# One group per expert for transposes, way back, scatter and gather; 4-KB pieces for gate and up rows

## The chip, the cores and the metric

The kernel runs on 1 core of one Trainium2 chip. The metric is device time in microseconds (us) of one execution; a kernel's time is the median over its runs. Engines are named as the profile names them: PE (TensorE matmul), PEld (TensorE weight load), DVE (VectorE), ACT (ScalarE), POOL (GpSimd), SP (SyncE, which issues nearly all DMAs).

## What is computed

256 positions of width 1024 pass through two blocks of two layers each. The first block and the attention parts of the second are untouched; the change lies in the mixture of experts that ends each layer of the second block:

```python
def grouped_moe(x, w_router, b_router, w_gate, w_up, w_down):
    scores = softmax(x @ w_router + b_router)
    ...  # group of 4 experts with the largest top-2 sum, then top 2 experts in it, renormalised -> gate (256, 16)
    y = zeros_like(x)
    for e in range(16):
        h = silu(x @ w_gate[e]) * (x @ w_up[e])      # 1024 -> 512
        y = y + gate[:, e:e+1] * (h @ w_down[e])     # 512 -> 1024
    return y
```

followed by `x = layer_norm(sqrt(2) * x + y)`. All weights are float32; one expert has 6.3 MB of them.

## The kernel before

**Weights.** All weights of the kernel come as one list of units of 512 KB in the order of their use. `load_ahead` (L262) issues the load of the next unit on SP as soon as a room (a 512-KB buffer in SBUF) is free in program order; `close` gives rooms back after the matmuls that read them. `hold(n)` keeps the next n rooms that come free away from the loads, and `take` hands them out for other tiles. An expert has 12 units: 4 pairs of gate and up (two blocks k of 128 rows by 512 columns each, so 2 KB in one piece) and 4 of down (128 rows by 1024 columns, 4 KB in one piece). The expert weights are used as they land, without the split into two parts that the other weights get.

**Router and gather.** `router` computes gates and, for each expert, a place among at most 64 (`CAP`) for each of its positions. `greater` and `lesser` split x into two parts `xn` for exact gathering. `gather(q)` makes `xgs[q]`, the transposed inputs of the four experts of group q: `select(q)` builds the one-hot `pick` on DVE, then four pieces of 8 matmuls each (L1845) go into a bank and are copied out by ACT or DVE in turn. Gather 0 runs ahead of the experts, gathers 1 to 3 are generators that `tick` moves on between units of the experts' matmuls.

**Experts.** `into(e)` multiplies the 64 gathered rows by gate and up: 4 steps u of two k each; gate goes to rows 0 to 63 of a bank and up to rows 64 to 127, so that the two matmuls use the two column halves of the array (64 columns each, L1936). `turn(e)` transposes the result (4 transposes, L1950), ACT applies silu (L1952), DVE multiplies (L1953). `down(e)` multiplies by the down weights (L1961), and ACT and DVE evict the result in two parts (L1967, L1968). `way_back(e)` makes the matrix that scatters back: POOL `pk` (L1862), 2 transposes (L1867), two DVE operations (L1870, L1871). `scatter(e)` adds the result to the four accumulators with 8 matmuls (L1977).

**Order.** The engines run in program order, written out by hand. The loop takes into(e+1) and then down(e). `turn(e)` is hooked behind step u = 0 of into(e+1), `scatter(e-1)` behind u = 2, `way_back(e+1)` comes by ticks behind u = 3, and pieces of a gather lie between steps. In experts 1, 4 and 8 a gather is started, and all its four pieces fall into into(e+1).

**Banks.** PSUM has 8 banks: 4 accumulators, and here 3 of kind `mm` (into, down) and 1 of kind `tp` (turn, way_back, gather). All tp users thus share one bank, each waiting until the one before has been read out. In layer 0, `memory` also uses tp late in the loop: from e = 12 it loads `stage` from ACT's queue and transposes it for the next layer.

Of the kernel before, what the change touches and what calls it, by code (L numbers as in the profile page):

```python
# [69 lines left out]
def the_kernel(  # L70
# [194 lines left out]
    def load_ahead(upto=None):  # L265
        units, loads, spare = now["units"], now["loads"], now["spare"]
        while spare and len(spare) > wanted_spare():
            give([spare.pop()])
        while len(loads) < min(len(units), upto or len(units)) and free:
            at = free.pop(0)  # L270
            w, c0, n, k0, m, _, _ = units[len(loads)]
            r = block(at, [UNIT], name="raw")[:, :m * n].rearrange("p (k n) -> p k n", n=n)
            nc.sync.dma_start(r, w[k0 * P:(k0 + m) * P, c0:c0 + n].rearrange("(k p) n -> p k n", p=P))
            loads.append((r, at))
            now["busy"].append(at)
# [1375 lines left out]
    def memory_attention(l, cs, xt, ready, memT, KT):  # L1651
        (memT, mem_rooms), (KT, KT_rooms) = memT, KT
        nxt, renew = start_norm(l, 1, split=False)
        with tc.tile_pool(name=f"xa{l}", bufs=1, reuse_waits="tile") as mp:
# [52 lines left out]
            gs = out_product(ot, renew, *([[gs[j, h]] for h in range(NH)] for j in range(2)), hurry=True)  # L1707
            hold(4)
            give(V_rooms + qT_rooms + KT_rooms + o_rooms)
            return nxt, gs  # L1710

    def moe(l, cs, xt, ready, turns, less_room):
        xg_rooms, xn_rooms = [], take(4, 4)
        xT = lambda h, k: xt[k // 4][:, k % 4, h * P:(h + 1) * P]
        later, whole, before, ones, numbers, order, earlier, alpha, wr, tr, sp = cs
        with tc.tile_pool(name=f"moe{l}", bufs=1, reuse_waits="tile") as mp:
# [6 lines left out]

            xn = [[block(r, [D], FR, "xn") for r in xn_rooms[i::2]] for i in range(2)]

            def greater(h):

                for j in range(2):
                    nc.scalar.activation(xn[0][h][:, j * 512:(j + 1) * 512], x[h][j], AF.Copy)

            def lesser(h, j):
                hi, lo = (t[h][:, j * 512:(j + 1) * 512] for t in xn)
                nc.vector.tensor_sub(lo, x[h][j], hi.bitcast(FT))

# [96 lines left out]
            def gather(q):  # L1831
# [3 lines left out]
                pick = picks[q]  # L1835
                if q % 2:
                    xg_rooms.extend(take(2, 2))
                xgs[q] = [block(r, [4, 4, CAP], name="xg") for r in (xg_rooms if q % 2 else pair_rooms[:2])]
                yield from wait(GW[0] if q else 0)
                for i in range(4):  # L1840
                    p = bank("tp" if q else "mm").rearrange("p (k e s) -> p k e s", k=2, s=CAP)
                    for k in range(2):
                        for h in range(NH):
                            for part in range(2):
                                nc.tensor.matmul(p[:, k].rearrange("p e s -> p (e s)"),  # L1845
                                                 xn[part][h][:, (2 * i + k) * P:(2 * i + k + 1) * P],
                                                 pick[:, h].rearrange("p e s -> p (e s)"), start=h == part == 0,
                                                 stop=h == part == 1)
                    o = xgs[q][i // 2][:, i % 2 * 2:i % 2 * 2 + 2]
                    if i % 2:  # L1850
                        nc.vector.tensor_copy(o, p)
                    else:
                        nc.scalar.activation(o, p, AF.Copy)  # L1853
                    yield from wait(2 if q else 0)
                if q == 3:
                    give(xn_rooms)

            def way_back(e):
# [5 lines left out]
                yield from wait(WB)  # L1864
# [3 lines left out]
                bk = mp.tile([P, NH, P], FR, name="back", bufs=2)  # L1868
                gw = mp.tile([P, 1], FT, name="gw", bufs=2)
# [3 lines left out]
                yield  # L1873

# [110 lines left out]
            turns.close()  # L1985
            turns.enter_context(banks(mm=3, tp=1))
            nc.scalar.activation(t2()[:, :1], gates[:, 0, 0:1], AF.Silu)
# [9 lines left out]

            spawn(way_back(0))
            into(0)
            for e in range(16):  # L2000
                if e in (0, 6):
                    hold(2)
                if e in (7, 15):
                    give(xg_rooms)
                    xg_rooms.clear()
                if e in (1, 4, 8):
                    gs.append(spawn(gather(len(gs))))
                if e == ME[0] and l == 0:
# [10 lines left out]
                if e == 15:  # L2019
# [4 lines left out]
                    break  # L2024
                if e % 4 == 3:
                    finish(gs[-1])
                wt = spawn(way_back(e + 1))
                into(e + 1, {0: lambda: turn(e), 2: lambda: e and scatter(e - 1)})
                finish(wt)
                down(e, (lambda: turn(15)) if e == 14 else None)  # L2030
# [91 lines left out]
```

## Time and profile before

| | |
|---|---|
| median of 3 runs | 2220.94 us (2216.73 to 2223.05) |
| profiled execution | 2218.42 us, its span 2216.7 us |
| PE busy, share of the span | 2132.8 us, 96% |
| DVE, ACT, POOL busy | 1139.0, 910.7, 177.0 us |
| HBM read | 487.34 MB |
| the largest PE groups of the experts | L1936 242.7 us (x1024), L1961 119.3 us (x512) |

Where rows show a time line, the columns are start, duration (from the first start to the last end of a merged group), engine, line, operation, out<-in, partitions*columns of the weights, the operand's shape, count and, in brackets, idle time of the engine before it and what ended it. A float32 matmul of the experts is recorded as two, so that a step u has 8 records of L1936 and down has 16 of L1961. Matmul ends are modelled; starts are the safer number. Rows of windows give the busy time of each engine, the granted clock, the DMA share and GB/s.

### The profile page before, as it was taken

Reading aid. Unit: us, or ns where it says so; the run is one execution under the profiler, and the core shown is the slowest. Engines: PE = TensorE matmul, PEld = TensorE weight load, DVE = VectorE, ACT = ScalarE, POOL = GpSimd, SP = SyncE. Lnnn points to the kernel's source line nnn. Section 1 sums busy time; section 2 is a strip of 40 time slices with the busy share of each in tenths; the row PEclk is TensorE's granted clock in tenths of the full one; section 3 lists DMA queues with packets and bytes.
Section 4 is the critical chain, followed back from the end, with each engine's and each line's share of the span. In section 5 each row is a group of like instructions: output and inputs, shape, how many; then the busy total and the mean of one; then the engine's idle time right before and its main releaser. Section 6 shows DMA issues by size and latency. Waiting matters only on the chain. (4 is left out here: it accounts for less than half of the span.)

```text
span 2216.7 us, 29473 instructions
## 1 busy us (share of the span) xinstructions
PE 2132.8 (96%) x11117; PEld 1569.8 (71%) x11117; DVE 1139.0 (51%) x2022; ACT 910.7 (41%) x1448; POOL 177.0 (8%) x230
## 2 busy tenths in 40 slices
PE   8999989999999999899999999998999999989997
PEld 7778878788888888788788887873333687953332
DVE  6545786654554547875554457651111558441112
ACT  5435655454454447564544454531111454421111
POOL 1000200200000002101100001101000102010000
PEclk9999999999999999999999999999999999999999
DMA  7655553555546555535666464778998946589996
GB/s 249 195 177 153 163 153 110 175 183 186 181 156 210 188 172 154 162 105 158 224 205 194 153 186 159 249 251 307 393 394 300 353 126 219 185 308 381 395 393 246
DMA packets 240076, 490.49 MB, mean 221 GB/s; under 512 B 17538, under 2 KB 44850, under 8 KB 239922
## 3 DMA queue, kind: packets, MB, share of 16 engines
q1 hardware_dynamic: 239634, 487.42, 65.1%
q8 instruction: 92, 1.51, 0.3%
q10 hardware_dynamic: 288, 1.05, 0.1%
q14 instruction: 62, 0.51, 0.1%
HBM read 487.34 MB, written 1.07 MB: 220 GB/s over the span
## 5 line engine op out<-in xcount | busy, mean ns | idle before, releaser
L285 DVE TENSOR_TENSOR wlo<-raw,whi 128x1024 fp32r<-128x1024 f32 x524 | 633.8, 1227 | 300.7 <-ACT whi L311 297.9
L311 ACT ACTIVATE whi<-raw 128x1024 fp32r<-128x1024 f32 x524 | 540.7, 1051 | 299.8 <-PE tp L360 117.5
L1936 PE MATMUL mm<-raw,xg 128*64 128x512 f32 x1024 | 242.7, 602 | 7.9 <-PEq L1992 7.2
L358 PE MATMUL accB<-whi,xt 128*128 128x512 f32 (+3 forms) x448 | 176.2, 393 | 0.0
L360 PE MATMUL accB<-whi,xt 128*128 128x512 f32 (+3 forms) x448 | 166.0, 370 | 0.0
L359 PE MATMUL accB<-wlo,xt 128*128 128x512 f32 (+3 forms) x448 | 165.8, 370 | 0.0
L1936 PEld LDWEIGHTS mm<-raw,xg 128*64 128x64 f32 x1024 | 69.6, 137 | 132.8 <-issue 121.5
L358 PE MATMUL tp<-whi,xt 128*128 128x512 f32 (+1 forms) x384 | 143.4, 373 | 0.0
L360 PE MATMUL tp<-whi,xt 128*128 128x512 f32 (+1 forms) x384 | 143.4, 373 | 0.0
L359 PE MATMUL tp<-wlo,xt 128*128 128x512 f32 (+1 forms) x384 | 142.7, 372 | 0.0
L358 PE MATMUL mm<-whi,xt 128*128 128x512 f32 (+1 forms) x320 | 121.0, 378 | 1.4 <-DVE nbias L720 0.7
L1961 PE MATMUL mm<-raw,t 128*64 128x512 f32 x512 | 119.3, 607 | 0.5 <-DMA raw<-in_w_down_dram 0.5
L360 PE MATMUL mm<-whi,xt 128*128 128x512 f32 (+1 forms) x320 | 118.3, 370 | 0.0
L359 PE MATMUL mm<-wlo,xt 128*128 128x512 f32 (+1 forms) x320 | 117.7, 368 | 0.0
L1941 ACT ACTIVATE t<-mm 128x512 f32<-128x512 f32 x32 | 19.1, 597 | 187.5 <-PE mm L1936 187.5
L360 PEld LDWEIGHTS accB<-whi,xt 128*128 128x128 f32 x448 | 84.5, 189 | 15.1
L358 PEld LDWEIGHTS accB<-whi,xt 128*128 128x128 f32 x448 | 84.6, 189 | 13.6 <-issue 1.0
L359 PEld LDWEIGHTS accB<-wlo,xt 128*128 128x128 f32 x448 | 84.8, 189 | 11.8
L1870 DVE TENSOR_SCALAR back<-tp 128x256 fp32r<-128x256 f32 x32 | 13.6, 424 | 149.2 <-PE tp L1867 149.2
L610 DVE SCALAR_TENSOR_TENSOR t<-tp,ss,t 128x512 f32<-128x512 f32 (+1 forms) x48 | 33.8, 704 | 104.2 <-PE tp L360 104.2
L359 PEld LDWEIGHTS tp<-wlo,xt 128*128 128x128 f32 x384 | 72.1, 188 | 13.5
L360 PEld LDWEIGHTS tp<-whi,xt 128*128 128x128 f32 x384 | 72.1, 188 | 13.2
(520 smaller groups left out, 4007.7 us busy)
## 6 DMA issues: line engine op xcount, KB each, us to landing
raw<-in_w_gate_dram SPq DMA_DIRECT2D x128, 512.0 KB
raw<-in_w_up_dram SPq DMA_DIRECT2D x128, 512.0 KB
raw<-in_w_down_dram SPq DMA_DIRECT2D x128, 512.0 KB
raw<-in_w_in_dram SPq DMA_DIRECT2D x120, 512.0 KB
raw<-in_ffn_w_gate_dram SPq DMA_DIRECT2D x88, 512.0 KB
raw<-in_ffn_w_up_dram SPq DMA_DIRECT2D x88, 512.0 KB
raw<-in_ffn_w_down_dram SPq DMA_DIRECT2D x88, 512.0 KB
raw<-in_w_out_dram SPq DMA_DIRECT2D x32, 512.0 KB
```

The source lines that it names most:

```text
L285: eng.tensor_sub(lo, r, hi.bitcast(FT))
L311: nc.scalar.activation(hi, r, AF.Copy)
L358: nc.tensor.matmul(o, xh, wh, start=first, stop=False)
L359: nc.tensor.matmul(o, xh, wl, start=False, stop=False)
L360: nc.tensor.matmul(o, xl, wh, start=False, stop=last)
L610: nc.vector.scalar_tensor_tensor(ss[h], o, factor(h), ss[h], op0=OP.mult, op1=OP.mult)
L1870: nc.vector.tensor_scalar(bk, tp, 0.0, None, op0=OP.is_gt)
L1936: nc.tensor.matmul(p[half(i)], xgs[e // 4][k // 4][:, k % 4, e % 4], W.whole(k, i), start=k == 0, stop=k == KD - 1)
L1941: nc.scalar.activation(c[e], p, AF.Copy)
L1961: nc.tensor.matmul(p[half(j)], uu[e][:, f], W.whole(f)[:, j * 512:(j + 1) * 512], start=f == 0, stop=f == 3)
```

## The change

- `between` is hooked behind u = 1 of into(e+1) and holds, in this order: turn(e), way_back(e+1), scatter(e-1), and one piece of a gather. The POOL part of way_back is now `gated_places`, issued ahead of into. Nothing is hooked behind u = 0, 2 and 3 any more.
- Gather 1 starts ahead of into(0), gathers 2 and 3 at e = 3 and 7; each puts one piece into each of four groups.
- Banks: 2 of mm and 2 of tp (3 and 1 before). `back` and `gw` have 3 buffers (2 before).
- The two rooms for odd gathers are taken once at the start of `moe` (`hold(6)` in place of `hold(4)`) and kept to e = 15; before, they were held at e = 0 and 6 and given back at e = 7 and 15.
- Gate and up units: partition p now gets rows 8p + k, so that its two rows k, k + 1 are neighbours in HBM: one piece of 4 KB where there were two of 2 KB, 16 KB from one partition's piece to the next. To match, `xn` holds the columns of x in the order k, m (from 8m + k), so that `greater` and `lesser` read x with a step of 8 elements.

```diff
-            w, c0, n, k0, m, _, _ = units[len(loads)]
+            w, c0, n, k0, m, _, whole = units[len(loads)]
             r = block(at, [UNIT], name="raw")[:, :m * n].rearrange("p (k n) -> p k n", n=n)
-            nc.sync.dma_start(r, w[k0 * P:(k0 + m) * P, c0:c0 + n].rearrange("(k p) n -> p k n", p=P))
+            if whole and m > 1:
+                nc.sync.dma_start(r, w[:, c0:c0 + n].rearrange("(p k) n -> p k n", p=P)[:, k0:k0 + m])
+            else:
+                nc.sync.dma_start(r, w[k0 * P:(k0 + m) * P, c0:c0 + n].rearrange("(k p) n -> p k n", p=P))
...
-            hold(4)
+            hold(6)
...
-        xg_rooms, xn_rooms = [], take(4, 4)
+        xg_rooms, xn_rooms = take(2, 2), take(4, 4)
...
+            eighths = lambda t, j: t.rearrange("p (k m) -> p k m", k=KD)[:, :, j * 64:j * 64 + 64]
...
-                    nc.scalar.activation(xn[0][h][:, j * 512:(j + 1) * 512], x[h][j], AF.Copy)
+                    nc.scalar.activation(eighths(xn[0][h], j), x[h][j].rearrange("p (m k) -> p k m", k=KD), AF.Copy)
...
-                yield from wait(GW[0] if q else 0)
                 for i in range(4):
+                    if i or q:
+                        yield
...
-                    yield from wait(2 if q else 0)
...
-            turns.enter_context(banks(mm=3, tp=1))
+            turns.enter_context(banks(mm=2, tp=2))
...
-            spawn(way_back(0))
-            into(0)
+            pk = gated_places(0)
+            rest_of = gather(1)
+            next(rest_of)
+            into(0, {1: lambda: (way_back(0, pk), next(rest_of))})
             for e in range(16):
...
-                if e in (1, 4, 8):
-                    gs.append(spawn(gather(len(gs))))
+                if e in (3, 7):
+                    rest_of = gather(e // 4 + 2)
+                    next(rest_of)
...
-                wt = spawn(way_back(e + 1))
-                into(e + 1, {0: lambda: turn(e), 2: lambda: e and scatter(e - 1)})
-                finish(wt)
+                pk = gated_places(e + 1)
+                def between():
+                    turn(e)
+                    way_back(e + 1, pk)
+                    if e:
+                        scatter(e - 1)
+                    next(rest_of, None)
+                into(e + 1, {1: between})
                 down(e, (lambda: turn(15)) if e == 14 else None)
```

## Rows read from the trace of the kernel before

**Rows 1.** Part 2 of the page: GB/s in 40 slices of 55.4 us

```profile
GB/s 249 195 177 153 163 153 110 175 183 186 181 156 210 188 172 154 162 105 158 224 205 194 153 186 159 249 251 307 393 394 300 353 126 219 185 308 381 395 393 246
```

**Rows 2.** Time line of PE, one expert of layer 1 without a gather

```profile
2017.03 1.89 PE L1936 MATMUL mm<-raw,xg 128*64 128x512 f32 x8
2018.85 0.66 PE L1950 MATMUL tp<-ident,t 128*128 128x128 f32 x4
2019.44 3.65 PE L1936 MATMUL mm<-raw,xg 128*64 128x512 f32 x16
2023.02 0.73 PE L1977 MATMUL accA<-t,back 64*128 64x512 f32 x4
...
2024.15 1.94 PE L1936 MATMUL mm<-raw,xg 128*64 128x512 f32 x8
2026.02 0.44 PE L1867 MATMUL tp<-ident,pk 128*128 128x128 f32 x2
2026.38 3.65 PE L1961 MATMUL mm<-raw,t 128*64 128x512 f32 x16
2029.87 1.89 PE L1936 MATMUL mm<-raw,xg 128*64 128x512 f32 x8
```

**Rows 3.** Time line of PE, the gather ahead of layer 1's experts and expert 1's

```profile
1970.99 4.05 PE L1845 MATMUL mm<-pick,xn 128*128 128x256 f32 x32
...
1997.60 1.89 PE L1936 MATMUL mm<-raw,xg 128*64 128x512 f32 x8
...
2001.13 1.21 PE L1845 MATMUL tp<-pick,xn 128*128 128x256 f32 x8 [1.06 <-DVE t L1953]
...
2008.28 1.21 PE L1845 MATMUL tp<-pick,xn 128*128 128x256 f32 x8
2010.17 1.21 PE L1845 MATMUL tp<-pick,xn 128*128 128x256 f32 x8 [0.69 <-ACT xg L1853]
```

**Rows 4.** Time line of PE, first group and end of layer 1's experts

```profile
1988.11 0.41 PE L1867 MATMUL tp<-ident,pk 128*128 128x128 f32 x2 [1.07 <-DVE t L1953]
...
2196.70 4.71 PE L1961 MATMUL mm<-raw,t 128*64 128x512 f32 x20
...
2203.03 0.49 PE L1977 MATMUL accA<-t,back 64*128 64x512 f32 x2 [0.26 <-DVE t L1968]
```

**Rows 5.** L273 on SP, 1979.5 to 2185: count, ns min/median/max, first and last start

```profile
L273 SPq DMA_DIRECT2D raw<-in_w_down_dram x56: 327/334/716, 1981.8 to 2181.6; - x56
L273 SPq DMA_DIRECT2D raw<-in_w_up_dram x50: 367/378/741, 1979.6 to 2170.8; - x50
L273 SPq DMA_DIRECT2D raw<-in_w_gate_dram x49: 367/383/1456, 1980.1 to 2169.5; - x49
```

**Rows 6.** Windows: start:end, length, PE, PEld, DVE, ACT, POOL, clock, DMA, GB/s

```profile
2134.50:2135.00 0.50, 0.50 (x6) 0.41 (x4) 0.00 (x0) 0.00 (x0) 0.00 (x0) 1.00 1.03 410
...
2158.50:2159.00 0.50, 0.50 (x6) 0.14 (x2) 0.00 (x0) 0.39 (x1) 0.00 (x0) 1.00 1.05 389
...
2190.00:2194.00 4.00, 4.00 (x24) 1.70 (x24) 0.51 (x2) 0.60 (x1) 0.00 (x0) 1.00 0.67 267
1742.00:1748.00 6.00, 5.06 (x38) 4.54 (x38) 5.86 (x13) 1.93 (x3) 1.60 (x1) 1.00 1.08 381
```

**Rows 7.** Time lines of SP, ACT and PE, end of layer 0's experts

```profile
1669.10 21.62 SPq L273 DMA_DIRECT2D raw<-in_w_down_dram  x4
...
1684.45 1.89 PE L1936 MATMUL mm<-raw,xg 128*64 128x512 f32 x8
...
1684.82 1.11 ACTq L1358 DMA_DIRECT2D stage<-in_mem_dram  x2
...
1697.09 1.08 PE L1961 MATMUL mm<-raw,t 128*64 128x512 f32 x4 [0.47 <-DMA raw<-in_w_down_dram]
...
1734.64 4.72 PE L1961 MATMUL mm<-raw,t 128*64 128x512 f32 x20
```

**Rows 8.** Groups by line, DVE in 1480 to 1500 us

```profile
L1733 DVE TENSOR_TENSOR xn<-x,xn 128x512 fp32r<-128x512 f32 x4 | 2.6, 677 | 0.0
```

More of the change, by code (lines that the diff above doesn't have):

```diff
@@ L1724, in moe @@
             xn = [[block(r, [D], FR, "xn") for r in xn_rooms[i::2]] for i in range(2)]
+            eighths = lambda t, j: t.rearrange("p (k m) -> p k m", k=KD)[:, :, j * 64:j * 64 + 64]
             def greater(h):
                 for j in range(2):
-                    nc.scalar.activation(xn[0][h][:, j * 512:(j + 1) * 512], x[h][j], AF.Copy)
+                    nc.scalar.activation(eighths(xn[0][h], j), x[h][j].rearrange("p (m k) -> p k m", k=KD), AF.Copy)
             def lesser(h, j):
-                hi, lo = (t[h][:, j * 512:(j + 1) * 512] for t in xn)
-                nc.vector.tensor_sub(lo, x[h][j], hi.bitcast(FT))
+                hi, lo = (eighths(t[h], j) for t in xn)
+                nc.vector.tensor_sub(lo, x[h][j].rearrange("p (m k) -> p k m", k=KD), hi.bitcast(FT))
             def router():
@@ L1835, in gather @@
                 pick = picks[q]
-                if q % 2:
-                    xg_rooms.extend(take(2, 2))
                 xgs[q] = [block(r, [4, 4, CAP], name="xg") for r in (xg_rooms if q % 2 else pair_rooms[:2])]
-                yield from wait(GW[0] if q else 0)
                 for i in range(4):
+                    if i or q:
+                        yield
                     p = bank("tp" if q else "mm").rearrange("p (k e s) -> p k e s", k=2, s=CAP)
@@ L1853, in gather, with gated_places @@
                         nc.scalar.activation(o, p, AF.Copy)
-                    yield from wait(2 if q else 0)
                 if q == 3:
                     give(xn_rooms)
-            def way_back(e):
+                yield
+            def gated_places(e):
                 pk = mp.tile([P, NH, 2, CAP], FT, name="pk", bufs=2)
@@ L1863, in way_back @@
                                             gates[:, h, e:e + 1], None, op0=OP.mult)
-                yield from wait(WB)
+                return pk
+            def way_back(e, pk):
                 tp = tbank()[:, :2]
@@ L1867, in way_back @@
                     nc.tensor.transpose(tp[:, h], pk[:, h].rearrange("p a s -> p (a s)"), ident)
-                bk = mp.tile([P, NH, P], FR, name="back", bufs=2)
-                gw = mp.tile([P, 1], FT, name="gw", bufs=2)
+                bk = mp.tile([P, NH, P], FR, name="back", bufs=3)
+                gw = mp.tile([P, 1], FT, name="gw", bufs=3)
                 nc.vector.tensor_scalar(bk, tp, 0.0, None, op0=OP.is_gt)
@@ L1872, in way_back @@
                 back[e] = bk, gw
-                yield
             ys = [[bank(ACC[h]) for _ in range(2)] for h in range(NH)]
@@ L1996, in moe @@
                     slow_expert(e, rest)
-            spawn(way_back(0))
-            into(0)
+            pk = gated_places(0)
+            rest_of = gather(1)
+            next(rest_of)
+            into(0, {1: lambda: (way_back(0, pk), next(rest_of))})
             for e in range(16):
-                if e in (0, 6):
-                    hold(2)
-                if e in (7, 15):
+                if e == 15:
                     give(xg_rooms)
-                    xg_rooms.clear()
-                if e in (1, 4, 8):
-                    gs.append(spawn(gather(len(gs))))
+                if e in (3, 7):
+                    rest_of = gather(e // 4 + 2)
+                    next(rest_of)
                 if e == ME[0] and l == 0:
@@ L2024, in moe @@
                     break
-                if e % 4 == 3:
-                    finish(gs[-1])
-                wt = spawn(way_back(e + 1))
-                into(e + 1, {0: lambda: turn(e), 2: lambda: e and scatter(e - 1)})
-                finish(wt)
+                pk = gated_places(e + 1)
[6 more added lines that the diff above has]
+                into(e + 1, {1: between})
                 down(e, (lambda: turn(15)) if e == 14 else None)
```

## The prediction

> **What bounds the kernel now.** I read the slices first, to find the two stretches of the experts: near 395 GB/s from about 1500 to 1750 us (layer 0) and 1980 to 2195 us (layer 1), 150 to 250 GB/s in most others [rows 1]. PE and the loads both work there without a break, so I then took PE's time line (what is an expert made of, and does PE wait?) and SP's (when is the last weight loaded?).
>
> PE first. A plain expert takes 2029.87 - 2017.03 = 12.84 us [rows 2]: step u0 1.82, turn 0.59, u1 and u2 3.58, scatter 1.13, u3 1.87, way_back 0.37, down 3.49 (start to start). A step that runs on from one like it costs about s = 1.72, half of down less a little. So every change between 64-column matmuls and the rest costs 0.10 to 0.15: 10.76 for six steps where 6s is 10.32. PE waits for no weight in such an expert.
>
> Then the loads. Layer 1's experts need 192 units. From 1979.6, the first load that waited for an expert to free a room, SP issues 56 + 50 + 49 = 155 of them [rows 5]; 37 are loaded or under way by then. At 394 GB/s [rows 1] a unit takes 1.33 us, and an expert's twelve 16 us: longer than PE's 12.84. PE lives on the stock of 37. Behind the last down unit, issued at 2181.6 [rows 5], come only two 512-KB rows of the norm; from 2190 to 2194 us 267 GB/s, or 1.07 MB, flow [rows 6], just these rows. So the last weight lands at about 2190.0, and down(15) ends at 2196.70 + 4.71 = 2201.4 [rows 4]. Layer 1 thus has two ends close together: PE's, and the loads', 10 us earlier. Whatever PE saves beyond that must come from faster loads.
>
> Layer 0 has a third actor. SP's four down loads take 21.62 us from 1669.10: SP stands until the `stage` load, which ACT issues at 1684.82, only when expert 12 begins (1684.45), has landed. The down weight behind it makes PE wait at 1697.09 [rows 7]. From there the loads set the pace to the end of down(15) at 1734.64 + 4.72 = 1739.4.
>
> **The change part by part.**
>
> (a) One group in place of three. In between remain u0u1 (2s + 0.10) and u2, u3 and down without a break (4s + 0.05): 10.47 for 10.76, a saving of 0.29 for each of the 14 experts e = 1 to 14. Inside the group way_back follows turn, and scatter follows way_back; whether their first weight load is then hidden no row shows: 0 to 0.18 more. I take 0.39, 5.5 us a layer (4.1 to 6.6).
>
> (b) Gathers. Expert 1, with its gather, takes 2017.03 - 1997.60 = 19.43 [rows 3, 2], 6.59 more than a plain one. Four pieces follow there, of 1.14 each, with stalls of 1.06 and 0.69 for the only tp bank (turn's, until DVE has multiplied; the third piece's, until ACT has copied) and a further change of form. After: a piece in a group that exists anyway, 1.01 (a quarter of gather 0 [rows 3]) to 1.14; I take 1.08, 4.3 for four. The stall of 1.06 goes: the piece takes turn's bank again, but way_back (0.3) and scatter (1.1) lie between. What is late next there is nothing. 2.27 saved for each of three gathers: 6.8 us a layer (6.1 to 7.6).
>
> (c) The first experts. The wait of 1.07 of way_back(0) behind turn(0) [rows 4] goes; but e = 0 has no scatter to cover its piece, so some 0.7 of stall comes. With (a)'s 0.29 and one more group in into(0): 0.5 us saved.
>
> So PE needs 12.8 us less in layer 1 (10.7 to 14.7); by the start of expert 12 in layer 0, three plain experts less, 11.6.
>
> (d) New waits. Turn, scatter and down get their inputs from ACT and DVE as before; scatter(e-1) now comes some 5 us behind down(e-1), and its eviction takes 2203.03 - 2201.41 = 1.6 us [rows 4]. With two mm banks into and down take turns, and each bank is read out while the other fills. POOL's `pk` is issued an expert ahead, `select` on DVE in front of the multiplication by more than 2 us. I cost these at nothing; the cover is u0 and u1, 3.5 us, and u2 and u3 ahead of down.
>
> (e) Pieces of 4 KB. Within a period of twelve units the rate swings between about 389 and 410 GB/s [rows 6]; the 410 lasts about a third of it, which fits the 4 down units of 4-KB pieces. So a gate or up unit would cost 1.28 us for 1.35, if 16 KB between pieces is no matter. The nearest row of pieces that lie apart is w_in's, 2 KB every 10 KB: 381 GB/s [rows 6], 2% under 389. I take u = 1.30 for a mean unit, with bounds 1.28 and 1.35 (nothing gained, spaced as w_in).
>
> [...]
>
> (f) Two rooms less at the start: two loads come later, so 157 follow where 155 did.
>
> (g) Strided reads. `greater` and `lesser` read x 32 bytes apart. A `lesser` takes 677 ns [rows 8]; two of eight lie on the router's path. Between unchanged and doubled: 0 to 1 us a layer; I take 0.4. (The skill's "SBUF — State Buffer", section "SBUF: two separate sides", has a penalty for each access that leaves a 16-byte line; the trace before has no such read, and by that rule the upper end would hold.)
>
> **Layer 1.** Start-up and latency of the loads: 2190.0 - 1979.6 - 155 x 1.33 = 4.3. After: last weight at 1979.6 + 4.3 + 157 x 1.30 = 2188.0, its matmuls 1.1 more: 2189.1. PE by itself: 2201.4 - 12.8 = 2188.6. The later rules: 12.3 saved, less 0.4: 11.9. At 1.28 PE rules and 12.4 are left; at 1.33, 7.2; at 1.35, 4.
>
> **Layer 0.** Expert 12 starts 11.6 earlier, and with it the `stage` load that lets SP go on. From there to the wait at 1697.09 are 12.6, to the next unit 1.4, then 27 units at the loads' pace, and 1.1 behind the last: 15.1 + 27 x 1.30 = 50.2, for 1739.4 - 1684.45 = 54.9 before. 4.7 more saved (5.4 at 1.28, 3.4 at 1.35). PE alone would need some 45, so its own gain there, and two banks for `memory`'s transposes, are hidden behind the loads. Less 0.4 for (g) and 1.0 (0 to 3) because the next layer's wk_x weights, which landed before they were needed, now come just in time: 14.9.
>
> The sum against the profiled execution: 2218.4 - 11.9 - 14.9 = 2191.6. The runs' median is 2.5 above that execution, inside their spread of 6; I forecast 2192.
>
> **The rivals.**
> 1. The pieces bring no rate (u = 1.33 or more): layer 1 then ends with its loads, 7.2 or less saved, layer 0 14.1 or less: 2197 to 2202. For it: in the trace size of piece and spacing differ together, and only the rate is seen, not the unit. Against: 410 comes once a period.
> 2. The group keeps its boundary costs inside (weights of full width cannot be loaded ahead of time there either) and a piece stays at 1.14: (a) gives nothing, (b) only its two stalls, 1.9 a gather. Layer 1 saves 6, layer 0 9: 2203. For it: a piece behind scatter in expert 1 costs as much as any. Against: a switch costs PE 0.10 to 0.15 at both ends [rows 2], and two of three pairs go.
> 3. Slower: pieces 16 KB apart meet in the same part of HBM. With g for a gate or up unit, u = (8g + 4 x 1.28) / 12, and the whole gain is (216 - 157u) + (50 - 27u) = 266 - 184u, the two layers' sums above with u left open: it is gone at u = 1.45, g = 1.53, which is 343 GB/s. At 300 GB/s (g = 1.75, u = 1.59) layer 1 loses 216 - 157 x 1.59 = -34; layer 0 would then wait for its loads before expert 12 too, and lose about as much: 2285. Against: w_in's spaced pieces keep 381.
> 4. The change doesn't do what it says: PE waits inside the group (a bank, `back`), and what is saved comes back: no change, 2217.
>
> **How the numbers follow.** Forecast 0.60, rival 1 0.15, rival 2 0.12, rival 3 0.06, rival 4 0.07. The forecast's own range is 2184 (PE saves 14.7 a layer, u = 1.28) to 2198. The range of 8 in 10 takes in rivals 1 and 2: 2183 to 2207. A difference of 0.3%, 6.7 us, is about the least that a measurement of this kernel tells from none. Faster by more: 0.88, within: 0.06, slower: 0.06.
>
> **What would show it.** In the profile after: a plain expert of layer 1 of 12.3 to 12.6 us; each group turn, way_back, scatter, piece without an idle bracket but in e = 0; experts with a piece 1.0 to 1.2 longer, none at 19; the DMA rate flat near 400 to 410 with no swing; the last weight of layer 1 at most 2 us before PE needs it; SP's stand for `stage` still there but about half as long. Wrong it would be if PE waits for raw weights through the middle of the experts (rival 3), or if the idle brackets move into the group.

## The result, and the profile after

| | before | after |
|---|---|---|
| median of the runs | 2221.99 us (2216.73 to 2223.74, 4 runs) | 2193.02 us (2189.24 to 2195.14, 4 runs) |
| ratio | | 0.9875, 95% interval 0.9853 to 0.9896 |
| profiled execution | 2218.4 us, span 2216.7 | 2189.24 us, span 2187.5 |
| experts of layer 0, first `into` to end of down(15) | 1502.34 to 1739.36: 237.0 | 1501.99 to 1721.8: 219.8 |
| from there to layer 1's experts | 238.3 | 239.9 |
| experts of layer 1 | 1977.64 to 2201.41: 223.8 | 1961.65 to 2172.55: 210.9 |

The changed kernel is 29 us faster, 1.25%. The forecast was 2192.0. The rows of the table add up: 17.2 from layer 0's experts, 12.9 from layer 1's, less 1.6 between them, and 0.7 at the two ends make the 29.2 between the spans. The new line numbers: the matmuls of gate and up are L1942, of down L1967; turn is L1956, way_back L1874, scatter L1983, a gather's piece L1849, the loads of raw weights L275 and L277, the stage load L1362 and the memory's transposes L1369.

The slices of the page after, GB/s in 40 slices of 54.7 us, against [rows 1]: the full slices of the two stretches of the experts now stand at 405 to 409, where 393 to 395 stood; the 361 is the slice with SP's stand for `stage`, told of below.

```profile
GB/s 251 190 178 152 170 154 116 164 170 189 183 158 209 188 177 166 170 100 170 175 226 189 180 175 125 264 170 317 409 409 361 390 150 203 192 254 405 409 409 302
```

The time line of PE after, layer 1: an expert with a piece of a gather, and a plain one (start, length, engine, line, operation, idle time before it in brackets). It answers to [rows 2].

```profile
2104.92 3.60 PE L1942 MATMUL mm<-raw,xg 128*64 128x512 f32 x16
2108.46 0.66 PE L1956 MATMUL tp<-ident,t 128*128 128x128 f32 x4
2108.95 0.38 PE L1874 MATMUL tp<-ident,pk 128*128 128x128 f32 x2
2109.26 0.74 PE L1983 MATMUL accA<-t,back 64*128 64x512 f32 x4
2109.84 0.63 PE L1983 MATMUL accB<-t,back 64*128 64x512 f32 x4
2110.40 1.21 PE L1849 MATMUL tp<-pick,xn 128*128 128x256 f32 x8
2111.54 3.65 PE L1942 MATMUL mm<-raw,xg 128*64 128x512 f32 x16
2115.02 3.60 PE L1967 MATMUL mm<-raw,t 128*64 128x512 f32 x16
2118.46 3.60 PE L1942 MATMUL mm<-raw,xg 128*64 128x512 f32 x16
...
2130.85 3.60 PE L1942 MATMUL mm<-raw,xg 128*64 128x512 f32 x16
```

One group per expert, no idle bracket in it. A plain expert takes 2130.85 - 2118.46 = 12.39 us, where it took 12.84; one with a piece takes 2118.46 - 2104.92 = 13.54, and the piece itself 2111.54 - 2110.40 = 1.14. Inside the group turn takes 0.49, way_back 0.31 and scatter 1.14 from start to start, for 0.59, 0.37 and 1.13 before.

The only bracket inside a group is at e = 0, which has no scatter (against [rows 4], where way_back waited 1.07):

```profile
1975.19 1.20 PE L1849 MATMUL tp<-pick,xn 128*128 128x256 f32 x8 [0.76 <-DVE t L1959]
```

Windows of the kernel after (start:end, length, busy PE, PEld, DVE, ACT, POOL, clock, DMA share, GB/s): 150 us in the middle of layer 1's experts, and the end of them. They answer to [rows 6].

```profile
2000.00:2150.00 150.00, 150.00 (x776) 62.22 (x776) 26.10 (x56) 21.12 (x38) 13.01 (x22) 1.00 1.03 409
2164.00:2168.00 4.00, 4.00 (x22) 1.44 (x20) 0.00 (x0) 0.60 (x1) 0.00 (x0) 1.00 1.02 409
2168.00:2172.00 4.00, 4.00 (x20) 1.10 (x18) 1.18 (x2) 1.07 (x2) 0.00 (x0) 1.00 0.67 266
```

The rate has no swing any more: 409 GB/s throughout, and a 512-KB load takes 524288 / 409 GB/s = 1.282 us. In the last window 266 x 4 = 1.06 MB flow, as much as the two 512-KB rows of the norm behind the last weight. Read as in the prediction, that one landed at about 2168.0. But a load lands in sixteen parts, and the trace marks the last weight's from 2167.0 to 2169.9: part of the rows is there before its end. Its last use ends at 2167.84 + 4.71 = 2172.55:

```profile
2167.84 4.71 PE L1967 MATMUL mm<-raw,t 128*64 128x512 f32 x20
```

The last weight's own matmuls take 1.1 us, so PE needs it at about 2171.4, 1.5 us after it was complete. No bracket names a weight here: layer 1's experts end with PE.

Layer 0's end is another matter. SP, ACT and PE after, against [rows 7]:

```profile
1664.56 14.10 SPq L277 DMA_DIRECT2D raw<-in_w_down_dram  x4
...
1672.82 3.60 PE L1942 MATMUL mm<-raw,xg 128*64 128x512 f32 x16
...
1673.24 0.89 ACTq L1362 DMA_DIRECT2D stage<-in_mem_dram  x2
...
1685.89 1.04 PE L1942 MATMUL mm<-raw,xg 128*64 128x512 f32 x2 [0.52 <-DMA raw<-in_w_gate_dram]
...
1719.42 1.08 PE L1967 MATMUL mm<-raw,t 128*64 128x512 f32 x4 [0.20 <-DMA raw<-in_w_down_dram]
```

SP's four down loads still take 14.10 us for the 4.17 they take elsewhere, because one of them waits for the `stage` load that ACT issues at 1673.24, when expert 12 begins (1672.82; here and below the loop's step e = 12, which opens with into(13)). Behind that PE waits for raw weights at 1685.89 and still at 1719.42.

### The profile page after: what moved, and what is told of

Read it like the earlier page. It is cut to its first block, busy times and chain, and to the rows that moved or that the text cites. A ratio compares the mean times of both kernels' runs of the same rounds, so it can differ in the third digit from the quotient of the medians.

```text
span 2187.5 us, 29458 instructions
## 1 busy us (share of the span) xinstructions
PE 2116.1 (97%) x11117; PEld 1572.7 (72%) x11117; DVE 1139.3 (52%) x2022; ACT 914.5 (42%) x1448; POOL 176.9 (8%) x230
## 3 DMA queue, kind: packets, MB, share of 16 engines
HBM read 487.34 MB, written 1.07 MB: 223 GB/s over the span
## 5 line engine op out<-in xcount | busy, mean ns | idle before, releaser
L1942 PE MATMUL mm<-raw,xg 128*64 128x512 f32 x1024 | 236.6, 600 | 8.1 <-PEq L1998 7.2
L1942 PEld LDWEIGHTS mm<-raw,xg 128*64 128x64 f32 x1024 | 72.0, 137 | 143.9 <-issue 132.7
L1974 DVE SCALAR_TENSOR_TENSOR t<-mm,gw,t 128x512 fp32r<-128x512 f32 x32 | 24.0, 751 | 222.4 <-ACT t L1973 222.4
L1967 PE MATMUL mm<-raw,t 128*64 128x512 f32 x512 | 116.5, 594 | 0.5 <-DMA raw<-in_w_down_dram 0.4
L364 PEld LDWEIGHTS accB<-whi,xt 128*128 128x128 f32 x448 | 84.5, 189 | 15.1
L363 PEld LDWEIGHTS accB<-wlo,xt 128*128 128x128 f32 x448 | 84.7, 189 | 11.8
L1967 PEld LDWEIGHTS mm<-raw,t 128*64 128x64 f32 x512 | 36.0, 137 | 74.0 <-issue 61.3
L363 PEld LDWEIGHTS tp<-wlo,xt 128*128 128x128 f32 x384 | 72.1, 188 | 13.5
```

Source lines behind the costliest of these rows:

```text
L363: nc.tensor.matmul(o, xh, wl, start=False, stop=False)
L364: nc.tensor.matmul(o, xl, wh, start=False, stop=last)
L1942: nc.tensor.matmul(p[half(i)], xgs[e // 4][k // 4][:, k % 4, e % 4], W.whole(k, i), start=k == 0, stop=k == KD - 1)
L1967: nc.tensor.matmul(p[half(j)], uu[e][:, f], W.whole(f)[:, j * 512:(j + 1) * 512], start=f == 0, stop=f == 3)
L1974: nc.vector.scalar_tensor_tensor(yl, p, gw, yh.bitcast(FT), op0=OP.mult, op1=OP.subtract)
```

## The experiments

The theory: PE's shorter experts and the faster loads are both needed, since each of them alone runs into the other; inside the group nothing waits because of the second tp bank and because way_back and scatter lie between turn and the piece. The rivals were rival 1 (the pieces bring no rate), rival 2 (the group saves nothing) and, for each part, that it does the whole by itself. All ratios are to the kernel before, on the same chip; differences to the changed kernel are worked out as (ratio - 0.9875) x 2220 us. Both ratios have an interval of 0.15 to 0.2% to either side, so such a difference is uncertain by some 6 us; what a part is worth is read from the rows. (Layer times are from the first `into` to the end of down(15) of the profiled execution.)

### The changed kernel with rows of 2 KB

```diff
-            w, c0, n, k0, m, _, whole = units[len(loads)]
+            w, c0, n, k0, m, _, _ = units[len(loads)]
-            if whole and m > 1:
-                nc.sync.dma_start(r, w[:, c0:c0 + n].rearrange("(p k) n -> p k n", p=P)[:, k0:k0 + m])
-            else:
-                nc.sync.dma_start(r, w[k0 * P:(k0 + m) * P, c0:c0 + n].rearrange("(k p) n -> p k n", p=P))
+            nc.sync.dma_start(r, w[k0 * P:(k0 + m) * P, c0:c0 + n].rearrange("(k p) n -> p k n", p=P))
```

(`greater` and `lesser` read x contiguously again, too.)

> The changed kernel with gate and up in rows of 2 KB as before (and x split without the step of 8); order and banks stay. My theory: PE's saving of 12.9 us in layer 1 needs the faster loads; with 1.33 us for a unit layer 1 ends with its loads again, 4.3 + 157 x 1.33 after its first load, some 5 us later than in the changed kernel, PE waits for raw weights in the last experts, and layer 0's end comes 27 x 0.05 = 1.4 us later; the router wins back 0.4 a layer. Sum: about 5.5 us slower than the changed kernel, 2198 to 2199. Rival: the loads keep ahead of PE in any case; then it is 0.8 us faster than the changed kernel, about 2192, and PE waits for nothing in layer 1.

Measured: 2201.44 us (5 runs), ratio 0.9918 (0.9903 to 0.9932), 9.5 us slower than the changed kernel where 5.5 were expected. Window and end of layer 1's experts:

```profile
2000.00:2150.00 150.00, 150.00 (x774) 61.62 (x772) 25.00 (x53) 21.33 (x38) 13.01 (x22) 1.00 1.04 393
```

```profile
2163.97 1.04 PE L1937 MATMUL mm<-raw,xg 128*64 128x512 f32 x2 [0.18 <-DMA raw<-in_w_gate_dram]
...
2182.33 1.08 PE L1962 MATMUL mm<-raw,t 128*64 128x512 f32 x4 [0.21 <-DMA raw<-in_w_down_dram]
2183.60 1.08 PE L1962 MATMUL mm<-raw,t 128*64 128x512 f32 x4 [0.20 <-DMA raw<-in_w_down_dram]
```

The rate is 393 GB/s, and in the last experts the brackets name DMA: the stock of loaded weights is used up and the loads set the end. Layer 1's experts take 216.8 us; the prediction's rule for the loads gives 2.56 + 4.3 + 157 x 1.33 + 1.1 = 216.8 (2.56 is the time from the first `into`, 1967.90, to the first load that waited for a room, 1970.46; it was 1.94 before, and the first row takes 5.35 us here for 3.65, at a granted clock of 0.68 for 1.00). So that rule holds, and the pieces of 4 KB are worth 5.9 us in this layer, 0.6 of it that first row. Layer 0 lost 4.1 (223.9 for 219.8). 1.0 of it is the first row of the experts, 6.36 us for 5.35 (granted clock 0.57 over the row, for 0.68); the other 3 lie in the tail, 52.1 us from the start of expert 12 for 49.0, where 27 loads of 0.05 make only 1.4. PE's first wait is already for expert 12's last down weight (1687.93), for the next gate weight in the changed kernel (1685.89), so one unit more, 1.33, goes at the loads' pace: the stock ran out one unit earlier. That is the size that was missed.

### The kernel before with pieces of 4 KB alone

```diff
+            if whole and m > 1:
+                nc.sync.dma_start(r, w[:, c0:c0 + n].rearrange("(p k) n -> p k n", p=P)[:, k0:k0 + m])
+            else:
+                nc.sync.dma_start(r, w[k0 * P:(k0 + m) * P, c0:c0 + n].rearrange("(k p) n -> p k n", p=P))
```

(with the reads of x that belong to it)

> The kernel before with the 4-KB pieces alone (and x split with the step of 8). My theory: PE sets the end of layer 1 there, so faster loads give it nothing; layer 0's end wins 27 x 0.05 = 1.4 us, the router loses 0.4 a layer: 2221, no change that can be measured, though the rate in the experts goes from 394 to 409 GB/s. Rival: the pieces are a gain by themselves: 10 us or more, 2211 or less.

Measured: 2216.81 us (11 runs), ratio 0.9996 (0.9986 to 1.0007): nothing.

```profile
2000.00:2150.00 150.00, 145.01 (x728) 57.33 (x728) 25.29 (x52) 20.64 (x37) 11.81 (x20) 1.00 1.00 397
```

The rate is 397 GB/s at a DMA share of 1.00, for 409 at 1.03 in the changed kernel: the loads could go faster but wait for rooms, which PE frees no sooner. Layer 1's experts take 226.8 us for 223.8. Their first 40 matmuls took 11.80 us for 8.80, which is the difference: the granted clock was 0.50, the lower level of 1.2 GHz, from 1974.7 to 1980.0. The same pieces are worth 9.5 us behind the other parts (by the ratios) and nothing without them.

### The kernel before with two banks for each kind alone

```diff
-            turns.enter_context(banks(mm=3, tp=1))
+            turns.enter_context(banks(mm=2, tp=2))
```

> The kernel before with two banks of each kind and nothing else. My theory: the stalls on the single tp bank go, 1.06 + 0.69 in each of three gathers and 1.07 at the first expert of a layer, 6.3 us a layer; layer 1 has 10 us of slack in its loads, layer 0 passes it on through the stage load: 12 to 13 us, 2209. A plain expert stays at 12.84 us. Rival: the stalls are only replaced by others in the old order (the piece behind turn waits for ACT or DVE anyway): less than 4 us, 2218 or more.

Measured: 2203.61 us (5 runs), ratio 0.9938 (0.9923 to 0.9952): 13.8 us, half of the whole. Layer 0's experts take 226.2 us (237.0), layer 1's 216.0 (223.8), and in layer 1 no piece or transpose waits for tp any more:

```profile
2034.23 1.20 PE L1845 MATMUL tp<-pick,xn 128*128 128x256 f32 x8
...
2041.36 2.15 PE L1845 MATMUL tp<-pick,xn 128*128 128x256 f32 x16
```

The first answers to the row of [rows 3] with its 1.06, the second to the one with 0.69. The `stage` stand shortens with the earlier start of expert 12, from 19.1 to 13.5 us. In layer 0's tail the banks do something that the prediction had put down to the loads. The kernel before, PE:

```profile
1710.27 0.66 PE L1365 MATMUL tp<-ident,stage 128*128 128x128 f32 x4 [1.41 <-DVE mem L441]
...
1714.88 0.41 PE L1867 MATMUL tp<-ident,pk 128*128 128x128 f32 x2 [1.50 <-DVE mem L441]
1716.23 0.63 PE L1365 MATMUL tp<-ident,stage 128*128 128x128 f32 x4 [0.94 <-DVE gw L1871]
1716.79 5.35 PE L1961 MATMUL mm<-raw,t 128*64 128x512 f32 x16
```

With two banks, PE:

```profile
1677.88 1.89 PE L1936 MATMUL mm<-raw,xg 128*64 128x512 f32 x8
...
1727.61 1.08 PE L1961 MATMUL mm<-raw,t 128*64 128x512 f32 x4 [0.21 <-DMA raw<-in_w_down_dram]
```

Before, PE waited 3.85 us for the one bank around `memory`'s transposes, then down took 5.35 us for 3.65 at a granted clock of 0.68, and from there to down(15) no bracket names a DMA: PE ended that layer, not the loads. With two banks 1.20 us of such waits are left, the loads do end the layer, and the tail takes 50.8 us for 54.9, which is what the prediction's 15.1 + 27 u gives at 1.33 (51.0).

### The changed kernel with one tp bank

```diff
-            turns.enter_context(banks(mm=2, tp=2))
+            turns.enter_context(banks(mm=3, tp=1))
```

> The changed kernel with three mm banks and one tp bank. My theory: the group stands on the two banks. way_back comes straight behind turn and waits some 1.07 us for the bank in every expert, the piece behind scatter waits little: 15 x 1.07 = 16 us a layer more on PE, of which layer 0 passes on about 12 and layer 1 all: 2219 to 2223, the whole gain gone. Rival: the time in the group is that of the weight loads, and a wait of 1 us is partly in it: 2205 or less.

Measured: 2229.3 us (5 runs), ratio 1.0047 (1.0033 to 1.0061): 38 us slower than the changed kernel and 10 slower than the one before. The same expert as above:

```profile
2087.31 3.60 PE L1942 MATMUL mm<-raw,xg 128*64 128x512 f32 x16
2090.85 0.66 PE L1956 MATMUL tp<-ident,t 128*128 128x128 f32 x4
2092.53 0.41 PE L1874 MATMUL tp<-ident,pk 128*128 128x128 f32 x2 [1.02 <-DVE t L1959]
...
2102.05 3.60 PE L1942 MATMUL mm<-raw,xg 128*64 128x512 f32 x16
```

14.74 us for 13.54: way_back stands behind turn until ACT and DVE have read turn's bank (1.02), and the other 0.18 come with the restart. The waits of layer 1 say it in one row (engine, who waits for whom: us, times, longest):

```profile
PE tp L1874 <- DVE t L1959: 15.5, 15, 1.1
```

So rival 4 has a place: with one bank the group is a loss, since it puts two users of that bank side by side which the old order kept apart. It was expected to give back the gain, not more: 16 us were put down for layer 1 and 12 for layer 0, and 21.4 (232.3 for 210.9) and 20.1 (239.9 for 219.8) were lost.

### The changed kernel with scatter moved back

```diff
-                    if e:
-                        scatter(e - 1)
-                into(e + 1, {1: between})
+                into(e + 1, {1: between, 2: lambda: e and scatter(e - 1)})
```

> The changed kernel with scatter taken out of the group and put behind u = 2, where it was. My theory: two things are lost. The change of form costs 0.10 to 0.15 us at both ends together in each expert: a plain expert of layer 1 goes from 12.39 to about 12.53. And scatter covered the piece's wait for turn's bank: in the experts with a piece the idle time of 0.76 us that now only e = 0 has comes back, 10 times a layer. About 0.14 x 14 + 7.6 = 9.6 us a layer, 2193 + 18 = 2211. Rival: scatter costs the same wherever it stands and the bank comes free in time: within 3 us of the changed kernel.

Measured: 2213.14 us (10 runs), ratio 0.9981 (0.9972 to 0.9991): 23.5 us slower than the changed kernel, 18 were expected. The time line of PE, two experts of layer 1, the second without a piece:

```profile
2131.88 1.21 PE L1849 MATMUL tp<-pick,xn 128*128 128x256 f32 x8 [0.71 <-DVE t L1959]
2133.03 1.94 PE L1942 MATMUL mm<-raw,xg 128*64 128x512 f32 x8
2134.89 0.74 PE L1983 MATMUL accA<-t,back 64*128 64x512 f32 x4
...
2141.23 3.60 PE L1942 MATMUL mm<-raw,xg 128*64 128x512 f32 x16
...
2153.77 3.60 PE L1942 MATMUL mm<-raw,xg 128*64 128x512 f32 x16
```

A plain expert takes 2153.77 - 2141.23 = 12.54 for 12.39: one more change between the 64-column matmuls and the rest, there and back, costs 0.15. An expert with a piece waits 0.71 besides, because nothing lies between way_back and the piece that takes turn's bank (8.0 us in 11 such waits of layer 1). The changed kernel has one such wait, of 0.76. That makes 14 x 0.15 + 8.0 - 0.8 = 9.3 of the 11.4 us that layer 1 lost (222.3 for 210.9); 1.4 more are the first row, 5.00 for 3.65 us. Scatter in the group is thus worth more as a cover than as a boundary saved. Layer 0 lost 10.1 as well (229.9).

### All four pieces of a gather in one group

```diff
-                    next(rest_of, None)
+                    for _ in range(4 if e % 4 == 2 else 0):
+                        next(rest_of, None)
-            into(0, {1: lambda: (way_back(0, pk), next(rest_of))})
+            into(0, {1: lambda: way_back(0, pk)})
```

> The changed kernel with all four pieces of a gather in one group (e = 2, 6, 10) and none in the others. My theory: with two tp banks the pieces can follow each other (each is copied out in 0.6 to 0.7 us while the next of 1.0 runs), so that spreading them one per expert gives nothing more than the banks and the group do: within 2 us of the changed kernel, the expert with four pieces 4.0 to 4.6 us longer than a plain one. Rival: the pieces wait for each other's copy, and spreading is what saved the stalls: 1 us or more a gather, 2199 or more.

Measured: 2189.24 us (4 runs), ratio 0.9876 (0.9861 to 0.9891), the changed kernel's time.

```profile
1998.90 4.12 PE L1849 MATMUL tp<-pick,xn 128*128 128x256 f32 x32
2002.95 3.65 PE L1942 MATMUL mm<-raw,xg 128*64 128x512 f32 x16
```

Four pieces in a row cost 4.05 without a wait (two banks, and ACT and DVE copy in turn). One piece in a group costs 1.14, so each that follows another costs (4.05 - 1.14) / 3 = 0.97. What the 0.17 of a lone piece are is not shown: the group ends with one change to 64 columns with or without a piece, and scatter takes the same 1.14 ahead of either. Three gathers a layer would save about 1.5 us so; layer 0's experts take 218.1 (219.8), layer 1's 211.1 (210.9), where the first row took 5.35 us for the changed kernel's 3.65 (granted clock 0.68 for 1.00 over the row) and ate the gain. Spreading the pieces brings nothing here by itself.

### The stage load one expert earlier

Layer 0's tail was left bound by its loads, so the next three ask what SP's stand is worth.

```diff
-ME = 9, 12, 20
+ME = 9, 11, 20
```

> The changed kernel with layer 0's load of stage (and the transposes behind it) one expert earlier, at e = 11. My theory: SP's stand of 12 us for that load sets the end of layer 0. Issued some 12 us earlier, it lands about when SP comes to the load behind it, the loads go on without a break, and layer 0's experts end with PE, not with their weights: 4 to 5 us sooner, 2188 to 2189. Rival: the loads that go on earlier meet other limits (rooms, the next layer's wk_x), and less than 1.5 us comes through.

Measured: 2200.03 us (5 runs), ratio 0.9917 (0.9902 to 0.9933): 9 us slower than the changed kernel (6.7 between the profiled executions: 3.5 in layer 0's experts, 1.7 in the first row of layer 1's, the rest around them). The theory fell. SP and ACT:

```profile
1650.28 16.58 SPq L277 DMA_DIRECT2D raw<-in_w_down_dram  x4
...
1661.42 0.86 ACTq L1362 DMA_DIRECT2D stage<-in_mem_dram  x2
```

The stage load is 11.8 us earlier, but so is the raw load that waits for it: SP runs ahead of the program by its stock, and the load that stands is one a few places behind `stage` in the program's order, wherever that is. The stand stays (16.58 for 14.10), and one expert more runs at the loads' pace behind it. Layer 0's experts take 223.3.

### The stage load from SP's own queue

```diff
-                    mt = spawn(memory(memT[0], "tp", 2, ME[2], apart=True))
+                    mt = spawn(memory(memT[0], "tp", 2, ME[2]))
```

> The changed kernel with the two stage loads of the memory issued by SP, in its own order among the raw loads, in place of ACT; nothing else is moved, least of all a raw load. Theory: SP's stand of 14 us is the wait of a raw load for a stage load on the other queue, which ACT can only issue when expert 12 begins. From SP it goes out in order, as soon as SP comes to it, and its rooms have been free since expert 9: no stand over 3 us behind expert 11, no dip of the transfers about 1670 to 1680, no wait of PE for raw weights in the last four experts of layer 0. These then end with PE: expert 12 starts at about 1672.8 as before, and the stretch behind it is four experts of 12.4 (one of them with nothing to turn), two groups of transposes and the end, some 45 us in place of 49.0: layer 0's experts take 215 to 216 us in place of 219.8, and layer 1's stay at 211. If the 1.6 us between the layers grows by no more than 1, 3 to 4 us faster than the changed kernel: a ratio of about 0.986 to the kernel before (0.9875 for the changed kernel). Rival A: SP stands for its own stage load just as long (for rooms or for something that it shares with earlier loads): 219 to 220 and 0.9875. Rival B: the stand goes, but what is gained in the experts is lost between the layers, where the weights of the next attention now come as late as before: layer 0 215, 4 us more until layer 1 begins, 0.9875.

Measured: 2198.61 us (5 runs), ratio 0.9918 (0.9905 to 0.9932): 9.5 us slower, none of the three cases that were written down. SP and PE:

```profile
1677.74 4.16 SPq L277 DMA_DIRECT2D raw<-in_w_down_dram  x4
...
1691.77 1.62 SPq L1362 DMA_DIRECT2D stage<-in_mem_dram  x2
```

```profile
1702.11 1.94 PE L1369 MATMUL tp<-ident,stage 128*128 128x128 f32 x8 [9.40 <-DMA stage<-in_mem_dram]
```

Windows of the same kernel, the wait and the stretch behind it:

```profile
1692.00:1702.00 10.00, 0.71 (x4) 0.00 (x0) 0.00 (x0) 0.00 (x0) 0.00 (x0) 0.72 1.02 409
1702.00:1707.00 5.00, 4.89 (x16) 2.34 (x16) 1.38 (x2) 1.19 (x2) 0.00 (x0) 0.53 1.03 410
```

The stand is gone (4.16 us) and the transfers never dip, as expected. But in SP's order the stage loads come behind the whole stock: at 1691.77 in place of 1673.24. PE stood 9.40 us until they had landed, and its granted clock in the 5 us behind was 0.53, near the lower level of 1.2 GHz: the transposes took 1.94 for 1.09. The expectation had costed when SP may issue, not when it comes to it.

### From SP, and one expert earlier

```diff
-ME = 9, 12, 20
+ME = 9, 11, 34
-                    mt = spawn(memory(memT[0], "tp", 2, ME[2], apart=True))
+                    mt = spawn(memory(memT[0], "tp", 2, ME[2]))
```

> The kernel before this one (stage loads from SP), with the loads spawned one expert earlier (at expert 11 in place of 12) and the transposes of the memory kept where the changed kernel has them (34 steps behind the spawn in place of 20). What the run before showed: from SP the stand is gone and the transfers never dip (409 GB/s from 1640 to 1702 us), but SP comes to the stage loads only behind all raw loads that stand ahead of them in its order, at 1691.77, and PE stood 9.40 us at the transposes until they had landed, then lost 1.3 and 0.85 us more in the two rows behind at a lower granted clock. Theory now: one expert earlier in SP's order is twelve loads of 1.28, 15.4 us: issued at about 1676.4, landed at about 1686.5, while PE comes to the transposes at about 1692.7. No wait of PE there, no dip of the clock, and the end of layer 0's experts is that of the run before less these 11.5: about 1717.1 us on its clock, layer 0's experts 215 to 216 us (219.8 in the changed kernel, 226 in the run before), the stretch between the layers 239 to 240 as before, layer 1 at 211: 4 us faster than the changed kernel, a ratio of about 0.9857 to the kernel before. Rival: the tail is bound by the raw loads all the same (the last down weights, issued to about 1704.9, land some 10 us later): PE waits for raw weights in the last two experts, and layer 0 takes 218 to 220, ratio 0.987. If SP stands again for rooms of the memory that an expert earlier are not yet free, layer 0 takes 222 or more.

Measured: 2188.02 us (4 runs), ratio 0.9864 (0.9848 to 0.9881). SP and PE:

```profile
1677.42 1.61 SPq L1362 DMA_DIRECT2D stage<-in_mem_dram  x2
...
1693.44 1.09 PE L1369 MATMUL tp<-ident,stage 128*128 128x128 f32 x8
...
1713.06 4.72 PE L1967 MATMUL mm<-raw,t 128*64 128x512 f32 x20
```

No wait of PE for a raw weight or for `stage` is left in layer 0's last four experts. They end at 1717.78 (1717.1 expected): 44.1 us from the start of expert 12 at 1673.70, for 49.0. Layer 0's experts take 214.9 us, 4.9 less than in the changed kernel, layer 1's 210.9 as there; the stretch between takes 240.4, 0.6 more. The span is 2184.1, 3.4 us under the changed kernel's. By the ratios it is 2.4 us faster, inside their intervals, so the total alone would not show it; the rows do. It is the fastest of the kernels here.

So the stand of SP in [rows 7] is a wait of a raw load for a DMA on the other queue. In the changed kernel it reads (engine, who waits for whom: us, times, longest):

```profile
SPq L277 <- DMA stage<-in_mem_dram: 12.4, 2, 12.0
```

The rooms of `stage` are no reason, since they are given back only after the transposes at 1695, and SP goes on at 1676.9. The semaphores in the traces show the reason, and it lies in the program. All these loads, on both queues, signal their landing on eight semaphores, taken in turn in the program's order, and a load waits until the one that had its semaphore before has landed. The two `stage` loads have 106 and 108; the raw load that gets 106 next waits for it from 1664.6 to 1676.9, and goes on when `stage` has landed (1676.8). It is the same in the kernel before and in the one with `stage` an expert earlier, there with 101.

## Why the prediction was right, point by point

**The bounds.** Right for layer 1. It had two ends close together, and whichever came later ruled: with 2-KB rows the loads (216.8 measured, 216.8 by the rule), with 4-KB pieces PE. That the pieces save nothing alone is the plainest proof. Before the change the loads' end was 8.5 us ahead of PE, not 10: the trace marks the last weight complete at 2191.8, not 2190.0. For layer 0 the bound was misread, as said below.

**(a) One group.** 12.39 us, a saving of 0.45 where 0.39 was taken and 0.47 was the upper bound: 0.30 at the boundaries for the 0.29 forecast, and 0.10 and 0.06 in turn and way_back from start to start, 0.16 of the up to 0.18 that was left open. That it is weight loads that are hidden there no row names. 14 x 0.45 = 6.3 us a layer for 5.5.

**(b) Gathers.** A piece costs 1.14, the upper bound, not 1.08; only one behind another piece is cheaper (0.97). Saved per gather: 6.59 - 4 x 1.14 = 2.03, 6.1 us a layer for 6.8. That the 1.06 would not come back was right, and for the reason given: without scatter between, 0.71 does.

**(c) First experts.** The new stall at e = 0 is 0.76 for the 0.7 taken. Layer 1's first stretch, up to into(2), took 19.96 us and now takes 21.58 with two pieces in it: less 2 x 1.14 that is 0.7 saved, for 0.5. By these rows (a) to (c) make 6.3 + 6.1 + 0.7 = 13.1; 12.9 were measured and 12.8 forecast. The misses of (a) and (b) cancel, which is luck.

**(d) New waits.** None appeared. The cover was the second bank; that `back` and `gw` have three buffers was not tried by itself.

**(e) Pieces.** u = 1.282, the lower bound, not 1.30. 4-KB pieces 16 KB apart run at 409 GB/s, as fast as down's contiguous units before, if the 410 of [rows 6] is theirs. The 381 of w_in [rows 6] was the wrong neighbour: 2-KB rows that lie next to each other ran at 389, so 2% at most go with the spacing there, and the step from 389 to 409 goes with the size of the piece. No run changes size and spacing one at a time. The Trainium skill ("DMA: Bandwidth & Descriptors", "Latency and other measured facts") has copies slowed where rows lie a large power of two apart: 103 GB/s a direction at a pitch of 4 MiB, 207 at 512 KiB, its smallest, and 214 at a padded pitch. No run here has such a pitch; at 16 KB the trace shows no loss, 409 GB/s. Rival 3 fell, and no wait for weights through the middle of the experts was seen. Rival 1's time, 2197 to 2202, is what the kernel with 2-KB rows takes (2201.4).

**(f) Two rooms less.** Not tried alone. The last weight of layer 1 is complete 1.5 us before PE needs it, inside the "at most 2 us". The way to place it, by the two rows that flow behind it, is 1.9 us too early here and 1.8 in the kernel before.

**(g) Strided reads.** Near the upper end for one operation, as taken for the path: `greater` takes 1132 ns a piece for 620, `lesser` 1070 for 677, and from the router's first matmul (L1743, now L1748) to `cnti` there are 14.2 us for 13.8 in both layers, 0.4 more; with 2-KB rows and contiguous reads it is 13.8 again. Groups of the two lines after (count, ns min/median/max, first and last start):

```profile
L1734 ACT ACTIVATE xn<-x x8: 1110/1132/1151, 1480.7 to 1945.9; 128x512 fp32r<-128x512 f32 x8
```

```profile
L1738 DVE TENSOR_TENSOR xn<-x,xn x8: 1061/1070/1109, 1483.4 to 1951.4; 128x512 fp32r<-128x512 f32 x8
```

The trace bears out the penalty of "SBUF — State Buffer", "SBUF: two separate sides", of the Trainium skill: 1.8 and 1.6 times, not quite the doubling taken as the upper end.

**Layer 1.** 12.9 saved between the first `into` and the end of down(15), where the forecast had 12.3 and let the loads rule (u = 1.30). In fact PE rules, as it said for u = 1.28.

**Layer 0.** 17.2 saved. Expert 12 starts 11.6 earlier, as forecast; the tail takes 49.0 for the 50.2 forecast (49.7 at u = 1.282). That it ends bound by its loads, with SP's stand cut from 21.62 to 14.10 (a third off, not a half), was right, and so was "PE alone would need some 45": with the stand gone it needs 44.1. Wrong was "from there the loads set the pace to the end of down(15)" for the kernel before, and with it that the second bank for `memory`'s transposes would be hidden. The sum's own 15.1 + 27 u gives 51.0 at 1.33, where 54.9 were measured. PE's waits for that bank (3.85) and the slower down behind them (1.7), shown above, had put PE 3.9 behind the loads. Of the 5.9 saved in the tail 4.1 come with the banks alone and 1.8 with the rest; the 4.7 forecast, all of it put down to the loads, came near by luck.

The stretch between the layers is 1.6 longer, for the 1.4 of the just-in-time weights and (g), but not by these two alone. ACT waits 2.62 us for a wk_x weight, where it waited for none before, and PE falls 2.5 us behind. It gets 1.4 of this back, since the kernel before ran the end of that part (1751 to 1755) at a granted clock of 0.57 and the changed one at 1.00. 0.6 are left when the router begins; (g) adds 0.3 to 0.4 and the 6.99 us from `cnti` to `into` (6.40 before) 0.6. No run says why the last is longer.

**The sum.** 29.2 measured between the profiled executions, 26.8 forecast: 0.6 more in layer 1's experts, 0.9 in layer 0's, and 0.9 around them (0.7 at the two ends less 1.6 between, for a forecast of 1.8 lost). The median of the runs lies 3.8 above the profiled execution, so that median and forecast meet within 1 us partly by chance.

What the experiments showed beyond it: the parts are not additive. Banks alone 13.8, pieces alone 0, the group and the banks without the pieces 18, the group and the pieces without the banks -10, all three 28. The banks and the pieces without the group were not run, so the group's own worth, 6.3 us a layer, stands on the rows alone.

## What to carry to other kernels

Where two limits lie within a few per cent of each other, look at both ends first: speeding up either alone buys little, and an experiment that does one part alone says nothing of its worth beside the other. When operations are put into one group, ask which of them share a buffer, and put work that needs no such buffer between them. Work out the sum for the kernel before as well: where it misses the time that is on record, a wait has been left out. Before a load is moved to another queue or another place in the program, read at what time that queue comes to it: a queue that runs ahead of the program has its whole stock in front of a new entry.

## What the runs showed of the hardware

- Weights in pieces of 4 KB, those of gate and up 16 KB apart in HBM, moved at 409 GB/s over 150 us; with gate and up in rows of 2 KB it was 393. The DMA share was 1.03 and 1.04, so the engines were full in both.
- The sixteen parts of one 512-KB load landed up to 2.8 us apart (2167.0 to 2169.9, layer 1's last weight), so the bytes that still flow do not tell when a load is complete.
- Reading fp32 with a step of 32 bytes made a 128x512 copy on ACT 1.8 times as long (620 to 1132 ns) and a subtraction on DVE 1.6 times (677 to 1070 ns).
- One more change from 64-column matmuls to full-width ones and back cost PE 0.15 us (scatter apart, 12.54 for 12.39).
- Behind a wait of 9.40 us PE's granted clock was 0.53 for 5 us, and eight transposes took 1.94 us for 1.09. Behind the 3.0 to 3.5 us for which PE waits ahead of layer 1's experts the first row took 3.65 us at a granted clock of 1.00 in three profiles (the changed kernel and the two with `stage` from SP) and 5.35 us at 0.68 in three others (2-KB rows, four pieces, `stage` an expert earlier).
